# Score products of a chunked linear-attention head pair: five separate blocks on TensorE, or one of three and one of two

## The chip, the core and the metric

The kernel runs on one core of one Trainium2 chip. The metric is device time in microseconds (us). Engines are named as in the profile: PE is TensorE (matmuls), PEld its weight loads, DVE VectorE, ACT ScalarE, POOL GpSimd, SP SyncE (DMA queue). Each engine takes its instructions from a queue of its own, in order, and waits there for what an instruction needs.

## The reference

One layer of a decoder trunk on 1024 tokens of width 1024, in float32. RMS norm, then `proj = h @ w_in` into eight groups of 1024 columns (xa, ga, q, f, v, g, m_a, m_b). Two token mixers run side by side: an RG-LRU on xa, and an HGRN2 (gated linear attention, 8 heads of 128 channels) on q, f, v. They are gated, summed, multiplied by `w_out` and added to x; then a squared-ReLU MLP of width 4096, a residual and a last norm. The part in question is HGRN2, which the reference writes over chunks of 32 tokens:

```
rel    = cum[:, :, :, None, :] - cum[:, :, None, :, :]          # cum: running sum of log f
decay  = where(causal, exp(minimum(rel, 0.0)), 0.0)
scores = einsum('bhtsk,bhsk->bhts', qc[:, :, :, None, :] * decay, kc)
o      = einsum('bhtk,bhkv->bhtv', qc * exp(cum), state) + einsum('bhts,bhsv->bhtv', scores, vc)
state  = exp(last)[..., None] * state + einsum('bhsk,bhsv->bhkv', k_to_end, vc)
```

So the score of tokens t >= s is a sum over 128 channels of q(t), k(s) and the product of the gates f between s and t.

## The kernel before, in words

Tokens go in two chunks c of 512; heads go in four pairs p. For every (c, p) the kernel projects v, xa, q and f, runs the RG-LRU, then `hgrn` (L381 to L559), then `gates` (L561), which projects g, m_b, ga and m_a and joins the branches. There are eight such rounds, about 107 us each; then come the output projection and the MLP, which the change does not touch. A projection is 48 matmuls of 128x512, three for every float32 product split in two (`mm3`, L113 to L117, so L115, L116 and L117 in the profile); their PSUM tiles are `pj_f`, `pj_g`, `pj_mb`, `pj_ga`, `pj_ma`. The weights are split by ACT (L76, high part `wH`) and DVE (L77, low part `wL`).

`hgrn` has no exponentials: it multiplies gates into q and k, and gets the scores level by level:
- own level (L385 to L404): tokens in twos. `q1` holds three versions of q. 32 small matmuls (32 stationary columns, 48 moving columns, L394) give the block `sc1`; a product with mask `mf` (tile `dd`) and a predicated copy take it up.
- `LEVELS = (2, 8)` (L425 to L462): `qa` and `qb` hold seven versions of q for groups of four cells of 2 and of 8 tokens; 32 small matmuls each (`sc2`, `sc8`), and three predicated copies each into `dd` (L438). After each level k is multiplied in place by the gates behind it (`kk`, L448) and q by those ahead.
- 32 (L475 to L487, 16 matmuls at L479, `sc32`) and 64 (L488 to L500, 8 matmuls at L497, `sc64`); ACT copies these blocks into `scT`, and POOL copies `dd` into `scT` with four instructions (L466).

So the block of one level reads `kk` and q as that level left them, and the next level's products overwrite `kk`. After that come transposes of `kk` (L525, `pk`), `pkv` (L531), the outputs `po` (L538, L541), the states `sn` on DVE (L547), and squares on ACT (L551).

What sets the order: a scheduler places every instruction on its engine's queue when the program is built, from the order in which the source makes them, priorities (the RG-LRU has 300, weight splits 400) and its own estimate of when inputs are ready; only the instructions under `keep` (norms and splits in the first round and in `first_norm`) are held in source order. So projection matmuls of `gates` stand on PE between the five score blocks. `bank("sc")` and `bank("hg")` are two PSUM banks each, and `pj` four; `mt(tag, ...)` gives one SBUF buffer for each tag, so a tile waits for the last reader of the tile that had its tag before. The second chunk's norm (`first_norm(1)`: L136 on ACT, L137 on DVE, L138 on POOL, L139 on DVE) begins in the last round of the first chunk.

Of the kernel before, what the change touches and what calls it, by code (L numbers as in the profile page):

```python
# [18 lines left out]
P = 128  # L19
D = 1024  # L20
S = 1024
T = 512
# [11 lines left out]
LEVELS = (2, 8)  # L34
# [7 lines left out]
def trunk(ctx: ExitStack, tc: tile.TileContext, x, wts, mlp, pv, gains, mask_f, mask_u, out):  # L42
    nc = tc.nc
    V, A, G, PE = nc.vector, nc.scalar, nc.gpsimd, nc.tensor
# [13 lines left out]
    def bank(tag, name):  # L58
        return ps.tile([P, 512], F32, tag=tag, name=name, bufs={"pj": 4, "sc": 2, "hg": 2}[tag])
# [129 lines left out]
    t3, t4, t5, t6 = (par[:, i, :] for i in range(3, 7))  # L189
# [37 lines left out]
    scT = mt("scT", "scT", (P, 8, P))  # L227
# [128 lines left out]

    def q_of(c, p, pp):

        q1 = mt("q1", f"q1{c}{p}", (P, 1792))[:, 0:1536].rearrange("p (a b) -> p a b", b=3)
        sg = mt("tmp", f"sq{c}{p}", (P, 2, T))  # L360
        r2 = lambda a: a.rearrange("p (a b) -> p a b", b=2)
        for s in range(2):
            b = slice(256 * s, 256 * s + 256)
            A.activation(sg[:, s, :], pp[s], AF.Sigmoid)
            V.tensor_tensor(out=q1[:, b, 0:2], in0=r2(sg[:, s, :]), in1=r2(pp[s]), op=ALU.mult)
        return q1

    def f_of(c, p, pp):
# [9 lines left out]
        V.tensor_scalar(ff, ff, F_MIN, 1.0, op0=ALU.max, op1=ALU.min)  # L378
        return ff, kk

    def hgrn(c, p, q1, f, kk, v):  # L381

        nm = f"{c}{p}"
        mul = lambda o, a, b: V.tensor_tensor(out=o, in0=a, in1=b, op=ALU.mult)  # L384
        mul(q1[:, :, 2], q1[:, :, 1], f[:, 1::2])  # L385
        dd = mt("dd", f"dd{nm}", (P, 8, 32))

        def blocks(rhs, name):

            pt = bank("sc", f"sc{name}_{nm}")[:, : 8 * 48].rearrange("p (n t) -> p n t", n=8)  # L390
            for n in range(8):
                for b in range(4):
                    k = 4 * n + b
                    PE.matmul(  # L394
                        pt[32 * b : 32 * b + 32, n, :], kk[:, 32 * k : 32 * k + 32], rhs(k), start=True, stop=True
                    )
# [7 lines left out]
        V.copy_predicated(dd[:, :, 1::2], mu[:, 0, :, 1::2], pt[:, :, :, 2])  # L404

        seg = mt("seg", f"seg{nm}", (P, 1536))
        f4 = f.rearrange("p (a b c) -> p a b c", b=4, c=2)
        qa = mt("qa", f"qa{nm}", (P, 1792)).rearrange("p (a b c) -> p a b c", b=7, c=2)
# [2 lines left out]
            q1.rearrange("p (a b) c -> p a b c", b=4)[:, :, :, 0:3:2],  # L411
            f4[:, :, :, 0:1].to_broadcast([P, 128, 4, 2]),
        )
        mul(kk[:, 0::2], kk[:, 0::2], f[:, 1::2])
        t4 = seg[:, 0:512]
        mul(t4, f[:, 0::2], f[:, 1::2])
        qb = mt("q1", f"qb{nm}", (P, 1792)).rearrange("p (a b) -> p a b", b=56)
        off = 512

        def take(n):  # L420
            nonlocal off
            off += n
            return seg[:, off - n : off]

        for li, cw in enumerate(LEVELS):  # L425
            g = 256 // cw
            t4 = t4.rearrange("p (a b) -> p a b", b=4)
            q4 = qa if li == 0 else qb.rearrange("p a (b c) -> p a b c", c=cw)

            mul(q4[:, :, 5, :], q4[:, :, 3, :], t4[:, :, 2:3].to_broadcast([P, g, cw]))  # L430
            mul(q4[:, :, 4:7:2, :], q4[:, :, 2:6:3, :], t4[:, :, 1:2].unsqueeze(3).to_broadcast([P, g, 2, cw]))
            pt = blocks(lambda k: q4[:, k * g // 32 : (k + 1) * g // 32, 1:7, :], str(cw))
            pt = pt.rearrange("p n (a x) -> p (n a) x", x=6 * cw)
            dg = dd.rearrange("p n (a x) -> p (n a) x", x=4 * cw)
            for d, a in ((1, 0), (2, 3), (3, 5)):
                w = (4 - d) * cw
                m_ = mu[:, 3 * li + d, :, :].rearrange("p n (a x) -> p (n a) x", x=4 * cw)
                V.copy_predicated(dg[:, :, d * cw :], m_[:, :, d * cw :], pt[:, :, a * cw : a * cw + w])  # L438
# [8 lines left out]
            k4 = kk.rearrange("p (a b c) -> p a b c", b=4, c=cw)  # L447
            mul(k4[:, :, 0:3, :], k4[:, :, 0:3, :], after.unsqueeze(3).to_broadcast([P, g, 3, cw]))  # L448
            if li == 0:
                o4 = qb[:, :, 0:32].rearrange("p a (b x) -> p a b x", b=4)  # L450
                i4 = lambda j: qa[:, :, j, :].rearrange("p (a b) c -> p a b c", b=4)
                A.copy(o4[:, :, :, 0:2], i4(0))
                for j in range(1, 4):
                    m_ = t4[:, :, 0] if j == 1 else before[:, :, j - 2]
                    m_ = m_.rearrange("p (a b) -> p a b", b=4).unsqueeze(3).to_broadcast([P, 32, 4, 2])
                    mul(o4[:, :, :, 2 * j : 2 * j + 2], i4(j), m_)
            else:
                mul(q4[:, :, 1, :], q4[:, :, 1, :], t4[:, :, 0:1].to_broadcast([P, g, cw]))
                mul(q4[:, :, 2:4, :], q4[:, :, 2:4, :], before.unsqueeze(3).to_broadcast([P, g, 2, cw]))
            nxt = take(g)  # L460
            mul(nxt, before[:, :, 0], after[:, :, 1])
            t4 = nxt  # L462
        tc_ = t4
        qv = qb[:, :, 0:32]
        for b in range(4):
            G.tensor_scalar(  # L466
# [5 lines left out]
                op1=ALU.add,  # L472
            )

        pt = bank("sc", f"sc32_{nm}")[:, :256].rearrange("p (n t) -> p n t", n=8)  # L475
        for n in range(8):
            for b in (0, 2):
                k = 4 * n + b
                PE.matmul(  # L479
                    pt[32 * b : 32 * b + 32, n, :],  # L480
                    kk[:, 32 * k : 32 * k + 32],
                    qb[:, k + 1, 0:32],
                    start=True,
                    stop=True,
                )
        for b in (0, 2):
            A.copy(scT[32 * b : 32 * b + 32, :, 32 * b + 32 : 32 * b + 64], pt[32 * b : 32 * b + 32, :, :])  # L487
        q8 = qv.rearrange("p (a e) c -> p a e c", e=2)  # L488
        k8 = kk.rearrange("p (a e c) -> p a e c", e=2, c=32)
        t8 = tc_.rearrange("p (a e) -> p a e", e=2)  # L490
        mul(q8[:, :, 1, :], q8[:, :, 1, :], t8[:, :, 0:1].to_broadcast([P, 16, 32]))
        mul(k8[:, :, 0, :], k8[:, :, 0, :], t8[:, :, 1:2].to_broadcast([P, 16, 32]))
        t64 = take(16)
        mul(t64, tc_[:, 0::2], tc_[:, 1::2])
        pt = bank("sc", f"sc64_{nm}").rearrange("p (n t) -> p n t", n=8)
        for n in range(8):
            PE.matmul(  # L497
                pt[0:64, n, :], kk[:, P * n : P * n + 64], qb[:, 4 * n + 2 : 4 * n + 4, 0:32], start=True, stop=True
            )
        A.copy(scT[0:64, :, 64:128], pt[0:64, :, :])  # L500
        q16 = qv.rearrange("p (a e d) c -> p a e d c", e=2, d=2)
        k16 = kk.rearrange("p (a e c) -> p a e c", e=2, c=64)
        t16 = t64.rearrange("p (a e) -> p a e", e=2)
        mul(k16[:, :, 0, :], k16[:, :, 0, :], t16[:, :, 1:2].to_broadcast([P, 8, 64]))
        qf = mt("qa", f"qf{nm}", (P, 1792))[:, 0:1024]
        qf5 = qf.rearrange("p (a b c d) -> p a b c d", b=2, c=2, d=32)
        A.copy(qf5[:, :, 0, :, :], q16[:, :, 0, :, :])
        mul(
            qf5[:, :, 1, :, :],
            q16[:, :, 1, :, :],  # L510
            t16[:, :, 0:1].unsqueeze(3).to_broadcast([P, 8, 2, 32]),
        )
        t128 = take(8)
        mul(t128, t64[:, 0::2], t64[:, 1::2])

# [110 lines left out]
    for c in range(NC):  # L626
# [6 lines left out]
        for p in range(NPAIR):  # L633
# [6 lines left out]
            q1 = q_of(c, p, project(c, f"q{c}{p}"))  # L640
            f, kk = f_of(c, p, project(c, f"f{c}{p}"))
# [407 lines left out]
```

## Time and profile before

| | |
|---|---|
| median of 3 runs | 1620.1 us (1618.43 to 1620.38) |
| the profiled execution | 1621.31 us, of which its span (first to last instruction) is 1619.5 us |
| PE busy | 1573.0 us, 9240 matmul records |
| DVE busy | 1211.3 us, 1751 instructions |
| ACT busy | 763.0 us, 1186 instructions |
| POOL busy | 66.8 us, 99 instructions |
| mean granted TensorE clock | 0.996 |

The page of the profile lists busy time by engine, the costliest groups of instructions, and the chain that ended last. The view of waits lists who waited for whom. The timeline lists instructions by start; a row has start, duration, engine, line, operation, out<-in, shapes, and in brackets the idle time before it and what ended that. Matmuls are pipelined, so a PE row overlaps the next: on PE the distance from start to start is what counts.

### The profile page before, as it was taken

Reading aid. Unit: us, or ns where it says so; the run is one execution under the profiler, and the core shown is the slowest. Engines: PE = TensorE matmul, PEld = TensorE weight load, DVE = VectorE, ACT = ScalarE, POOL = GpSimd, SP = SyncE. Lnnn points to the kernel's source line nnn. Section 1 sums busy time; section 2 is a strip of 40 time slices with the busy share of each in tenths; the row PEclk is TensorE's granted clock in tenths of the full one; section 3 lists DMA queues with packets and bytes.
Section 4 is the critical chain, followed back from the end, with each engine's and each line's share of the span. In section 5 each row is a group of like instructions: output and inputs, shape, how many; then the busy total and the mean of one; then the engine's idle time right before and its main releaser. Section 6 shows DMA issues by size and latency. Waiting matters only on the chain.

```text
span 1619.5 us, 23177 instructions
## 1 busy us (share of the span) xinstructions
PE 1573.0 (97%) x9240; PEld 1302.9 (80%) x9240; DVE 1211.3 (75%) x1751; ACT 763.0 (47%) x1186; POOL 66.8 (4%) x99
## 2 busy tenths in 40 slices
PE   7999999999999999999999997999999999999998
PEld 6788788788788788788787875888888878888886
DVE  5975956848763865947758688888878888888876
ACT  4643545436433544446335466677667732222113
POOL 0010100100100000000100010000000000000000
PEclk9999999999999999999999999999999999999999
DMA  6212213122243212222122362666666575666652
GB/s 238 92 66 91 92 66 104 67 92 91 79 168 132 92 68 90 92 77 93 66 92 91 111 228 78 252 244 244 243 248 249 221 286 206 257 258 250 257 213 104
DMA packets 57996, 246.51 MB, mean 152 GB/s; under 512 B 6688, under 2 KB 6816, under 8 KB 47136
## 3 DMA queue, kind: packets, MB, share of 16 engines
q1 hardware_dynamic: 56304, 239.27, 39.6%
q10 hardware_dynamic: 1584, 5.77, 1.0%
q8 instruction: 72, 1.18, 0.3%
q14 instruction: 36, 0.29, 0.1%
HBM read 185.24 MB, written 59.77 MB: 151 GB/s over the span
## 4 chain that ended last, share of the span: by engine, by line
PE 77%; DVE 17%; DMA 2%; ACT 2%; issue 2%; POOL 0%; DVEq 0%; POOLq 0%; SPq 0%; ACTq 0%
PE dX L115 3%; PE dX L116 3%; PE dX L117 3%; PE uX L115 3%; PE uX L117 3%; PE uX L116 3%; DVE wL L77 2%; PE pj_ga L117 2%; PE pj_ga L116 2%; PE pj_ga L115 2%; PE pv L115 2%; PE pv L117 2%; PE pv L116 2%; PE pj_f L117 2%; PE pj_ma L117 2%; PE pj_ma L116 2%
## 5 line engine op out<-in xcount | busy, mean ns | idle before, releaser
L77 DVE TENSOR_TENSOR wL<-raw,wH 128x1024 fp32r<-128x1024 f32 x160 | 194.3, 1215 | 150.2 <-ACT wH L76 146.1
L76 ACT CAST wH<-raw 128x1024 fp32r<-128x1024 f32 x160 | 167.8, 1049 | 166.6 <-issue 66.5
L963 DVE TENSOR_TENSOR acc<-acc,dX 128x512 f32<-128x512 f32 x128 | 85.1, 684 | 29.5 <-PE dX L117 28.6
L76 ACT CAST wA<-q 128x512 fp32r<-128x512 f32 x32 | 19.8, 622 | 134.1 <-PE dX L117 101.5
L963 DVE TENSOR_TENSOR acc<-acc,dY 128x512 f32<-128x512 f32 x64 | 43.4, 686 | 15.6 <-PE dY L117 14.5
L345 DVE RECIPROCAL rr<-rr 128x512 f32<-128x512 f32 x16 | 53.5, 3346 | 0.0
L823 ACT ACTIVATE b<-b 128x512 f32<-128x512 f32 x48 | 30.2, 630 | 37.4 <-DVE b L822 37.4
L115 PE MATMUL pv<-wH,hT0H 128*128 128x256 f32 x128 | 37.4, 292 | 0.0
L116 PE MATMUL pv<-wL,hT0H 128*128 128x256 f32 x128 | 37.0, 289 | 0.0
L117 PE MATMUL pv<-wH,hT0L 128*128 128x256 f32 x128 | 37.0, 289 | 0.0
L115 PE MATMUL pv<-wH,hT1H 128*128 128x256 f32 x128 | 36.5, 285 | 0.0
L117 PE MATMUL pv<-wH,hT1L 128*128 128x256 f32 x128 | 36.2, 283 | 0.0
L116 PE MATMUL pv<-wL,hT1H 128*128 128x256 f32 x128 | 36.2, 283 | 0.0
L311 DVE SCALAR_TENSOR_TENSOR xc<-xp,pvt,xc 128x512 f32<-128x512 f32 x48 | 33.1, 747 | 0.0
L551 ACT ACTIVATE on<-po 128x128 f32<-128x128 f32 x64 | 16.9, 277 | 33.5 <-PE po L541 33.2
L570 ACT ACTIVATE smb<-pj_mb 128x512 f32<-128x512 f32 x16 | 9.6, 597 | 45.3 <-PE pj_mb L117 45.1
L824 ACT ACTIVATE b<-b 128x512 f32<-128x512 f32 x48 | 30.0, 630 | 1.1
L77 DVE TENSOR_TENSOR wA<-q,wA 128x512 fp32r<-128x512 f32 x32 | 22.0, 688 | 10.1 <-ACT wA L76 9.7
L444 POOL TENSOR_SCALAR seg<-seg 128x128 f32<-128x128 f32 (+1 forms) x16 | 14.5, 906 | 360.6 <-DVE seg L384 360.6
L565 ACT ACTIVATE g<-pj_g 128x512 f32<-128x512 f32 x16 | 9.6, 598 | 37.4 <-PE pj_g L117 37.4
L384 DVE TENSOR_TENSOR seg<-seg 128x128 f32<-128x128 f32 (+2 forms) x96 | 27.0, 311 | 0.2
L117 PE MATMUL pj_ga<-hT1H,wL 128*128 128x512 f32 x64 | 26.6, 415 | 0.0
(1854 smaller groups left out, 5251.7 us busy)
## 6 DMA issues: line engine op xcount, KB each, us to landing
raw<-wts_in SPq DMA_DIRECT2D x160, 512.0 KB, 3.4
q<-mlp_in SPq DMA_DIRECT2D x64, 512.0 KB, 4.0
x<-x_in SPq DMA_DIRECT2D x8, 512.0 KB, 6.5
acc<-x ACTq DMA_DIRECT2D x8, 512.0 KB, 5.4
y_out<-acc SPq DMA_DIRECT2D x16, 256.0 KB, 2.0
xs<-x_in SPq DMA_DIRECT2D x8, 256.0 KB, 3.5
x<-xs SPq DMA_DIRECT2D x8, 256.0 KB, 2.2
x2s<-x_in SPq DMA_DIRECT2D x4, 512.0 KB, 4.4
```

Of the source, the lines that this page charges most:

```text
L76: keep(A.copy(h, src))
L77: keep(V.tensor_tensor(out=lo, in0=src, in1=h.bitcast(F32), op=ALU.subtract))
L115: PE.matmul(o, ah, bh, start=first, stop=False, **how)
L116: PE.matmul(o, ah, bl, start=False, stop=False, **how)
L117: PE.matmul(o, al, bh, start=False, stop=last, **how)
L311: V.scalar_tensor_tensor(xc[:, s, :], xp[:, j : j + T], pvt[:, PV_CW + 8 * j + u : PV_CW + 8 * j + u + 1], xc[:, s, :], op0=ALU.mult, op1= ...
L345: V.reciprocal(rec, rec)
L384: mul = lambda o, a, b: V.tensor_tensor(out=o, in0=a, in1=b, op=ALU.mult)
L551: A.activation(on[:, 4 * s + n, :], po[:, n * P : (n + 1) * P], AF.Square, accum_out=ssq[:, 4 * s + n : 4 * s + n + 1])
L823: A.activation(b[:, at, :], b[:, at, :], AF.Relu, scale=-1.0 if at == 2 else 1.0)
L824: A.activation(b[:, at, :], b[:, at, :], AF.Square)
L963: V.tensor_tensor(out=dst, in0=dst, in1=banks[bk, pr], op=op)
```

## The change

The five blocks become two groups. Levels 1, 2 and 8 (`sc1`, `sc2`, `sc8`) are issued one behind another, held (by a dependency for the scheduler alone, no wait on the chip) behind the last q product of level 8. Then all mask products and predicated copies follow. Levels 32 and 64 (`sc32`, `sc64`) are issued as a second group behind the last q product of level 64. For that, each level's keys are kept: `kk` stays as it was for level 1, `kb` is new for level 2, `kc` for level 8 and 32 (tag `tmp`), and `kk` is written again for 64. `qb` gets a tag of its own instead of `q1`'s; `qf` takes the products of level 64. ACT gets the copies of what is not multiplied (`kb`, `kc`, `kk`). `sc8` goes to a bank of tag `hg`. The sums, products, masks and matmuls are otherwise those of before. The products `level_q` and `sums` are the former loop's, taken out as functions. The core of the diff, where the last pairs of lines but one are operands of the matmuls of `sc32` and `sc64`, each under `together(..., behind)`:

```diff
+    def together(ins, behind):
+        no_sync = mybir.DependencyInfo(mybir.DependencyClass.NoSync, mybir.DependencyReason.DATA)
+        tc.add_manual_dep(ins.ins, behind.ins.name, no_sync, reason="together")
...
-        def blocks(rhs, name):
+        def blocks(k_, rhs, name, behind, tag="sc"):
...
-        pt = blocks(lambda k: q1[:, 16 * k : 16 * k + 16, :], "1").rearrange("p n (a b) -> p n a b", b=3)
-        d2 = dd.rearrange("p n (a b) -> p n a b", b=2)
-        mf2 = mf.rearrange("p (a b) -> p a b", b=2).unsqueeze(1)
-        mul(d2, pt[:, :, :, 0:2], mf2.to_broadcast([P, 8, 16, 2]))
-        V.copy_predicated(dd[:, :, 1::2], mu[:, 0, :, 1::2], pt[:, :, :, 2])
+        def own_block(pt):
+            pt = pt.rearrange("p n (a b) -> p n a b", b=3)
+            d2 = dd.rearrange("p n (a b) -> p n a b", b=2)
+            mf2 = mf.rearrange("p (a b) -> p a b", b=2).unsqueeze(1)
+            mul(d2, pt[:, :, :, 0:2], mf2.to_broadcast([P, 8, 16, 2]))
+            V.copy_predicated(dd[:, :, 1::2], mu[:, 0, :, 1::2], pt[:, :, :, 2])
+        def level_blocks(li, cw, pt):
+            pt = pt.rearrange("p n (a x) -> p (n a) x", x=6 * cw)
+            dg = dd.rearrange("p n (a x) -> p (n a) x", x=4 * cw)
+            for d, a in ((1, 0), (2, 3), (3, 5)):
+                w = (4 - d) * cw
+                m_ = mu[:, 3 * li + d, :, :].rearrange("p n (a x) -> p (n a) x", x=4 * cw)
+                V.copy_predicated(dg[:, :, d * cw :], m_[:, :, d * cw :], pt[:, :, a * cw : a * cw + w])
...
-        mul(kk[:, 0::2], kk[:, 0::2], f[:, 1::2])
+        kb = mt("kb", f"kb{nm}", (P, 2 * T))
+        A.copy(kb[:, 1::2], kk[:, 1::2])
+        mul(kb[:, 0::2], kk[:, 0::2], f[:, 1::2])
...
-        qb = mt("q1", f"qb{nm}", (P, 1792)).rearrange("p (a b) -> p a b", b=56)
+        qb = mt("qb", f"qb{nm}", (P, 1792)).rearrange("p (a b) -> p a b", b=56)
...
-        for li, cw in enumerate(LEVELS):
...
+        level_q(qa, t4, g0, c0)
+        before, after = sums(t4, g0)
+        kc = mt("tmp", f"kc{nm}", (P, 2 * T))
...
+        A.copy(k4(kc, c0)[:, :, 3, :], k4(kb, c0)[:, :, 3, :])
+        mul(k4(kc, c0)[:, :, 0:3, :], k4(kb, c0)[:, :, 0:3, :], after.unsqueeze(3).to_broadcast([P, g0, 3, c0]))
...
+        behind = level_q(q4, t4, g1, c1)
+        pt1 = blocks(kk, lambda k: q1[:, 16 * k : 16 * k + 16, :], "1", behind)
+        pt2 = blocks(kb, lambda k: qa[:, k * g0 // 32 : (k + 1) * g0 // 32, 1:7, :], str(c0), behind)
+        pt8 = blocks(kc, lambda k: q4[:, k * g1 // 32 : (k + 1) * g1 // 32, 1:7, :], str(c1), behind, "hg")
+        before, after = sums(t4, g1)
+        own_block(pt1)
+        level_blocks(0, c0, pt2)
+        level_blocks(1, c1, pt8)
+        mul(k4(kc, c1)[:, :, 0:3, :], k4(kc, c1)[:, :, 0:3, :], after.unsqueeze(3).to_broadcast([P, g1, 3, c1]))
...
+        A.copy(pairs(kk)[:, :, 1, :], pairs(kc)[:, :, 1, :])
+        A.copy(pairs(qf)[:, :, 0, :], q8[:, :, 0, :])
+        mul(pairs(kk)[:, :, 0, :], pairs(kc)[:, :, 0, :], t8[:, :, 1:2].to_broadcast([P, 16, 32]))
+        behind = mul(pairs(qf)[:, :, 1, :], q8[:, :, 1, :], t8[:, :, 0:1].to_broadcast([P, 16, 32]))
...
+                        kc[:, 32 * k : 32 * k + 32],
+                        qb[:, k + 1, 0:32],
...
+                    pt64[0:64, n, :], kk[:, P * n : P * n + 64], qf[:, P * n + 64 : P * n + P], start=True, stop=True
...
+        mul(halves(kk)[:, :, 0, :], halves(kk)[:, :, 0, :], t16[:, :, 1:2].to_broadcast([P, 8, 64]))
+        mul(halves(qf)[:, :, 1, :], halves(qf)[:, :, 1, :], t16[:, :, 0:1].to_broadcast([P, 8, 64]))
```

More of the change, by code (lines that the diff above doesn't have):

```diff
@@ L423, in take, with sums @@
             return seg[:, off - n : off]
-        for li, cw in enumerate(LEVELS):
[L426 to L438, printed above, removed]
+        def sums(t4, g):
             after = take(3 * g).rearrange("p (a b) -> p a b", b=3)
@@ L446, in hgrn @@
             mul(after[:, :, 0], t4[:, :, 1], after[:, :, 1])
[L447 to L459, printed above, removed]
@@ new lines, in hgrn @@
+        A.copy(o4[:, :, :, 0:2], i4(0))
+        for j in range(1, 4):
+            m_ = t4[:, :, 0] if j == 1 else before[:, :, j - 2]
+            m_ = m_.rearrange("p (a b) -> p a b", b=4).unsqueeze(3).to_broadcast([P, 32, 4, 2])
+            mul(o4[:, :, :, 2 * j : 2 * j + 2], i4(j), m_)
+        nxt = take(g0)
+        mul(nxt, before[:, :, 0], after[:, :, 1])
+        t4 = nxt.rearrange("p (a b) -> p a b", b=4)
+        q4 = qb.rearrange("p a (b c) -> p a b c", c=c1)
+        behind = level_q(q4, t4, g1, c1)
@@ L478, in hgrn @@
                 k = 4 * n + b
[L479 to L485, printed above, removed]
+                together(
+                    PE.matmul(
+                        pt[32 * b : 32 * b + 32, n, :],
+                        kc[:, 32 * k : 32 * k + 32],
+                        qb[:, k + 1, 0:32],
+                        start=True,
+                        stop=True,
+                    ),
+                    behind,
+                )
@@ L489, in hgrn @@
[L489 to L492, printed above, removed]
+        A.copy(scT[0:64, :, 64:128], pt64[0:64, :, :])
         t64 = take(16)
         mul(t64, tc_[:, 0::2], tc_[:, 1::2])
[L495 to L499, printed above, removed]
```

55 lines of the change are left out of this document (33 added, 22 removed).

## The prediction

> **What bounds the kernel now.** First the page, for the bound as a whole.
>
> ```profile
> span 1619.5 us, 23177 instructions
> ...
> PE 1573.0 (97%) x9240; PEld 1302.9 (80%) x9240; DVE 1211.3 (75%) x1751; ACT 763.0 (47%) x1186; POOL 66.8 (4%) x99
> ...
> PE 77%; DVE 17%; DMA 2%; ACT 2%; issue 2%; POOL 0%; DVEq 0%; POOLq 0%; SPq 0%; ACTq 0%
> ```
>
> PE is busy nearly all the time, so a gain must come from time in which PE stands or is badly filled, and the change touches only the score blocks. Hence the view of waits, cut to PE:
>
> ```profile
> PE sc L394 <- DVE qb L384: 5.0, 8, 0.6
> PE sc L394 <- DVE q L384: 4.1, 8, 0.5
> ...
> PE sc L479 <- DVE qb L384: 0.4, 1, 0.4
> ```
>
> Two of the five blocks wait visibly for DVE in each of the eight rounds, 9.5 us in all. The timeline of PE in one round (second chunk, second pair) says more; all rounds repeat it closely.
>
> ```profile
> 654.13 0.39 PE L115 MATMUL pj_g<-hT1H,wH 128*128 128x512 f32 x1
> ...
> 664.56 0.39 PE L116 MATMUL pj_g<-hT1L,wH 128*128 128x512 f32 x1
> 665.46 0.89 PE L394 MATMUL sc<-q,kk 128*32 128x48 f32 x64 [0.51 <-DVE q L384]
> ...
> 670.26 0.39 PE L116 MATMUL pj_mb<-hT1L,wH 128*128 128x512 f32 x1
> 670.74 0.89 PE L394 MATMUL sc<-qa,kk 128*32 128x48 f32 x64
> ...
> 675.44 0.89 PE L394 MATMUL sc<-qb,kk 128*32 128x48 f32 x64 [0.62 <-DVE qb L384]
> ...
> 680.26 0.70 PE L479 MATMUL sc<-qb,kk 128*32 128x32 f32 x32
> ...
> 682.88 1.12 PE L497 MATMUL sc<-qb,kk 128*64 128x64 f32 x16
> ...
> 685.66 0.49 PE L117 MATMUL pj_ga<-hT1H,wL 128*128 128x512 f32 x1
> 685.99 0.39 PE L115 MATMUL pj_ga<-hT1H,wH 128*128 128x512 f32 x1
> ```
>
> From the first row to the second are 46 steps of projection matmuls: 10.43 / 46 = 0.227 us each. And now DVE beside it:
>
> ```profile
> 664.53 0.88 DVE L384 TENSOR_TENSOR q<-q,f 128x512 f32<-128x512 f32 x1
> ...
> 667.02 0.43 DVE L384 TENSOR_TENSOR dd<-sc,mf 128x256 f32<-128x256 f32 x1
> 667.35 1.22 DVE L77 TENSOR_TENSOR wL<-raw,wH 128x1024 fp32r<-128x1024 f32 x1
> 668.48 0.45 DVE L404 COPY_PREDICATED dd<-mu,sc 128x128 f32<-128x128 uint8 x1
> 668.71 0.74 DVE L384 TENSOR_TENSOR kk<-kk,f 128x512 f32<-128x512 f32 x1
> ...
> 669.98 0.70 DVE L384 TENSOR_TENSOR qa<-qa,seg 128x512 f32<-128x512 f32 x1
> ...
> 672.76 0.47 DVE L438 COPY_PREDICATED dd<-mu,sc 128x192 f32<-128x192 uint8 x1
> 673.06 0.97 DVE L384 TENSOR_TENSOR kk<-kk,seg 128x768 f32<-128x768 f32 x1
> 673.93 0.30 DVE L438 COPY_PREDICATED dd<-mu,sc 128x128 f32<-128x128 uint8 x1
> 674.13 0.43 DVE L384 TENSOR_TENSOR qb<-qb,seg 128x256 f32<-128x256 f32 x1
> 674.47 0.29 DVE L438 COPY_PREDICATED dd<-mu,sc 128x64 f32<-128x64 uint8 x1
> 674.60 0.69 DVE L384 TENSOR_TENSOR qb<-qb,seg 128x512 f32<-128x512 f32 x1
> ...
> 678.89 1.22 DVE L384 TENSOR_TENSOR qb<-qb,seg 128x256 f32<-128x256 f32 x2
> ...
> 682.65 0.68 DVE L384 TENSOR_TENSOR qf<-qb,seg 128x512 f32<-128x512 f32 x1
> 683.25 1.22 DVE L77 TENSOR_TENSOR wL<-raw,wH 128x1024 fp32r<-128x1024 f32 x1
> 684.39 0.69 DVE L384 TENSOR_TENSOR kk<-kk,seg 128x512 f32<-128x512 f32 x1
> ...
> 687.45 0.35 DVE L547 SCALAR_TENSOR_TENSOR sn<-scar,seg,pkv 128x128 f32<-128x128 f32 x1 [1.25 <-PE pkv L531]
> 687.84 0.73 DVE L547 SCALAR_TENSOR_TENSOR sn<-sn,seg,pkv 128x128 f32<-128x128 f32 x2
> ```
>
> Set the ends of DVE's products against the starts of the blocks: 665.41 and 665.46; 670.68 and 670.74; 675.29 and 675.44; 680.11 and 680.26. Blocks start 0.05 to 0.15 us behind the product that they read, also where the profile names no wait. **So the score blocks go at DVE's pace**, and DVE has no idle time from the first of these rows to the last but two. What the change does to PE's order matters less than when DVE ends the last product of each group.
>
> **Part by part.** The order of the built programs gives the counts. From the start of `pj_f` the old blocks stand behind 119, 137, 150, 166 and 173 projection matmuls; the new group of three behind 163, the group of two behind 183 (the same in seven rounds; 184 in the last of the first chunk). The number of matmuls and their shapes stay.
>
> *PE.* Three of five entries and exits go. An entry costs 0.48 us from start to start where no wait is named (670.26 to 670.74), 0.25 over a step; the first step behind a small run is 0.33 (685.66 to 685.99), 0.10 over. But an entry is a gain only if DVE is ready.
>
> *When DVE has the input of group two.* From 664.53 to 684.39 the old order spends 19.86 us, with no gap. It holds every instruction that the new order puts ahead of group two, the split of the weight at 683.25 too, which now stands ahead of the last products; and one more, the product `qf` for the halves, which takes 683.25 - 682.65 = 0.60 and now comes later. That leaves 19.26.
>
> *What is added on DVE: chains.* The mask product and the predicated copies all write `dd`, so each waits for the one before. Before, other products stood between them and the next instruction started early: 0.33 behind the mask product of 0.43, 0.23 behind the copy of 0.45, then 0.30, 0.20 and 0.13 behind copies of 0.47, 0.30 and 0.29. Now the five and a sixth stand in a row. What a chained pair costs is seen at 687.45: 0.35, and 0.04 later the next. So 0.10 + 0.22 + 0.17 + 0.10 + 0.16 + 5 x 0.04 = 0.95 us. The bounds are 0 and about 1.2 (a chained product of small sums too); I take 0.95, as the `sn` row shows just this case.
>
> [...]
>
> *The sum for group two.* 664.53 + 19.26 + 0.95 + 0.08 (the last product's own end: 0.68 against its step of 0.60) + 0.15 to PE = **684.97**. The old program reaches the 64-block at 682.88 behind 173 matmuls; ten more make 682.88 + 2.27 = **685.15**. Gain 0.18 us a round, in seven rounds 1.3.
>
> *Does PE get there first?* The last product of group one moves: ahead of it come a weight split (1.13, from 667.35 to 668.48), two gate products with g (some 0.6 each, as 682.65 to 683.25 for the same size) and two small sums (at most 0.3 together); five mask operations go behind it (0.33 + 0.23 + 0.30 + 0.20 + 0.13 = 1.19). So 674.60 + 1.4 + 0.69 + 0.15 = 676.9 for `sc8`; PE is there by 664.56 + 44 x 0.227 + 0.48 + two blocks of at most 0.89 = 676.8. With 0.89 for the block and twenty steps, PE stands before group two at about 682.5, DVE serves it at 685.0. The 2.5 us of stall take what the three entries and the two old waits gave, so no price of an entry or of a switch inside a group changes the result as long as it is below that.
>
> *Last round of the first chunk.* There the next norm falls into the chain:
>
> ```profile
> 418.36 0.14 DVE L137 TENSOR_SCALAR rstd_x<-rstd_x 128x1 f32<-128x1 f32 x1
> ...
> 423.23 1.28 DVE L139 SCALAR_TENSOR_TENSOR xn<-x,rstd_x,gain 128x1024 f32<-128x1024 f32 x1
> ```
> ```profile
> 418.64 1.01 POOL L138 TENSOR_TENSOR rstd_x<-rstd_x,mhalf 128x1 f32<-128x1 f32 x1 [0.23 <-DVE seg L384]
> ```
>
> Both DVE instructions now stand ahead of the mask product, with one small one between. DVE waits out POOL, 418.36 to 419.65 plus 0.15, less some 0.3 done meanwhile, 1.1; the norm product 1.2. In this round products stand between the copies again (some 0.6 of the chain back), and POOL's copies fall behind group two (up to 0.6 back). Net +1.1 to +1.7, against a gain of 0.18 and 0.36 of visible wait that this round had: about **0.8 us lost**.
>
> *Hidden work.* ACT gets three copies more a round:
>
> ```profile
> 673.29 1.05 ACT L76 CAST wH<-raw 128x1024 fp32r<-128x1024 f32 x1 [5.55 <-issue]
> ...
> 682.94 0.62 ACT L507 COPY qf<-qb 128x512 f32<-128x512 f32 x1
> ```
>
> Each is at most 0.62, and ACT idles 5.55 us there; the last that group two needs (`qf`) can start when `qb` is done, about 1.2 us before DVE's last product ends, so it is covered; without cover it would cost 0.62. Behind group two PE has four projections before `pk` instead of six, ACT makes the second `kT` behind one weight cast (1.05) that came later, while PE has ten matmuls for it instead of six (0.91 more): 0.1 us lost in each second-chunk round. In the first chunk PE's small runs split once or twice more, 0.10 each. Together about 0.8. SP's loads keep their order but for a few neighbours; weights are split before they are needed by more than 5 us.
>
> Total: -1.3 + 0.8 + 0.8 = **+0.3 us**. On the profiled span that is 1619.5 + 0.3 = 1619.8, its time 1621.6; the median shown is 1.2 us below that execution, so **1620.4 us**.
>
> **The rivals.** No change means within 0.2% (3.2 us), about what a measurement of this kernel can tell.
>
> *Chains cost nothing* (faster). Without the 0.95 the eight rounds gain 7.6 more: 1620.4 - 7.6 = 1612.8. It decides from 0.45 us a round. For it: a copy's duration in the row may hold time behind the instruction before it. Against: the `sn` rows. 0.17.
>
> *PE's switches are the limit, not DVE* (faster). [...] By rows: three entries of 0.25 and three exits of 0.10 and the two named waits (9.1 / 8 = 1.14) would go, 2.2 us a round, 17.5 in all: 1602.6. The 0.05 to 0.15 us between product and block, the same in all rounds, speak against it. 0.03.
>
> *POOL locks DVE out* (slower). POOL's four copies of `dd` now fall beside the split, and the last three products of group two:
>
> ```profile
> 679.14 2.16 POOL L466 TENSOR_SCALAR scT<-dd 32x256 f32<-32x256 f32 x4 [5.93 <-DVE dd L438]
> ```
>
> Beside them two products took 1.22 at 678.89; at 674.13 and 674.60 the same sizes made 0.34 + 0.69 = 1.03. So one of four copies cost 0.2, and the 19.86 holds that. [...] If DVE stood for all of the 2.16, less 0.2 to 0.8 held in the sum, a round would lose 1.4 to 2.0, all 11 to 16: 1631 to 1636; at half of it 1626. It decides from 0.4 us a round. 0.25 for at least that.
>
> *The change doesn't do what it says*: the built order on PE shows the blocks together, so nothing is given to it.
>
> **How the numbers follow.** Forecast 0.55, within 0.2%; faster 0.17 + 0.03 = 0.20; slower 0.25. Range: from the first rival to between the third's half and its full price, 1612.8 to 1628; own range of the forecast 1617.2 to 1623.6.
>
> **What would show it.** In the new profile: PE waiting at `sc8`, `sc32` or `sc64` for DVE, over 2 us a round; 0.15 us between DVE's last product and the 64-block; DVE with about 20.4 us from `q<-q,f` to that product's end, predicated copies 0.04 us behind each other; a longer wait in the last round of the first chunk. Wrong would be a second group that starts with no named wait (then entries count and it is faster), or copies of POOL over which `wL` and `kk` rows stretch (slower).

## The result, and the profile after

The changed kernel took 1627.5 us (median of 6 runs, 1624.7 to 1632.3) against 1618.5 us for the kernel before (6 runs, 1618.2 to 1620.4): a ratio of 1.005, 95% interval 1.004 to 1.0061. That lies inside the range, just below its upper end, and outside the forecast of no change. The profiled execution is the slowest of the six, 1632.3 us at a mean granted clock of 0.988; the other five had 0.991 to 0.993, so what follows is the dearest case.

From the page of the changed kernel (span; busy time by engine; the queue q8, which e2 and e8 tie to PE's instructions):

```profile
span 1630.5 us, 23238 instructions
...
PE 1577.3 (97%) x9240; PEld 1313.0 (81%) x9240; DVE 1216.0 (75%) x1751; ACT 775.5 (48%) x1210; POOL 63.7 (4%) x99
...
q8 instruction: 72, 1.18, 0.3%
```

The same 9240 matmul records take PE 4.3 us more, and the span grows by 11.0. So this is not only waiting: matmuls themselves got longer. (A small float32 matmul leaves two records, called passes here: the 32 matmuls of `sc8` are 64 passes.) The view of waits, PE of the changed kernel (engine, line, releaser: total us, times, longest):

```profile
PE sc L398 <- issue: 7.5, 4, 2.0
...
PE sc L525 <- DVE qf L388: 4.6, 5, 2.0
PE sc L513 <- DVE qb L388: 3.6, 4, 1.1
PE sc L398 <- DVE qb L388: 2.9, 8, 0.4
```

Before, the blocks waited 9.5 us for DVE. Now they wait 11.1 for DVE and 7.5 for "issue", that is, for nothing that the profile names. The two kinds stand in different places, as the timeline of PE shows. First chunk, first pair:

```profile
98.28 0.93 PE L513 MATMUL sc<-qb,kc 128*32 128x32 f32 x32 [1.04 <-DVE qb L388]
99.89 1.91 PE L525 MATMUL sc<-qf,kk 128*64 128x64 f32 x16 [0.67 <-DVE qf L388]
101.72 0.80 PE L115 MATMUL pj_ga<-hT0H,wH 128*128 128x512 f32 x1
102.32 0.63 PE L116 MATMUL pj_ga<-hT0L,wH 128*128 128x512 f32 x1
102.75 0.63 PE L117 MATMUL pj_ga<-hT0H,wL 128*128 128x512 f32 x1
...
684.63 0.63 PE L398 MATMUL sc<-qb,kc 128*32 128x48 f32 x40 [0.37 <-DVE qb L388]
687.23 0.71 PE L398 MATMUL sc<-qb,kc 128*32 128x48 f32 x24 [1.97 <-issue]
687.87 0.80 PE L116 MATMUL pj_mb<-hT1L,wH 128*128 128x512 f32 x1
```

Above the dots, PE stands before each half of group two and waits for DVE, as predicted. Behind it the projection steps are 0.43 us apart (102.32 to 102.75) instead of 0.227, and the 64-block takes 1.91 instead of 1.12. Below the dots is the second chunk, second pair (the round of the prediction): PE stops *inside* `sc8`, after 40 of its 64 passes, for 1.97 us, and the next projection is slow again, 0.80 instead of 0.39. The stretches of 3.41 us around both places, with busy time by engine and the granted clock in the last column but two:

```profile
96.51:99.92 3.41, 1.68 (x37) 1.06 (x36) 3.23 (x4) 1.22 (x3) 3.22 (x4) 1.00 0.43 143
99.92:103.33 3.41, 3.41 (x20) 3.00 (x21) 1.44 (x3) 1.79 (x4) 0.09 (x1) 0.50 0.04 16
683.60:687.01 3.41, 1.29 (x103) 1.05 (x90) 3.13 (x14) 0.00 (x0) 0.00 (x0) 1.00 0.27 106
687.01:690.43 3.42, 3.20 (x30) 2.60 (x31) 2.13 (x6) 0.45 (x1) 0.37 (x1) 0.50 0.02 5
```

PE is busy for 1.68 of 3.41 us, or 1.29, and in the 3.41 us that follow the clock is granted at 0.50. The changed kernel has such a stretch in each of the eight rounds; before, no round had one. At 0.50 a stretch of 3.41 us loses half of its work, some 1.7 us (an estimate). Over the whole of the prediction's round, `pj_f` to `poT`, the view of windows gives for before, then for changed:

```profile
637.56:710.76 73.20, 71.80 (x556) 58.31 (x555) 57.12 (x88) 36.47 (x64) 5.20 (x7) 1.00 0.22 76
645.39:720.27 74.88, 72.46 (x555) 59.62 (x554) 57.89 (x88) 37.97 (x67) 4.80 (x7) 0.98 0.23 73
```

Measured from the first matmul of `pj_f` to the first of `poT` (two rows of the timeline), a round takes:

| kernel | first chunk, us | second chunk, us |
|---|---|---|
| before | 74.0, 73.2, 73.2, 73.6 | 73.2, 73.2, 73.2, 73.3 |
| changed | 75.6\*, 74.8\*, 74.8\*, 75.2\* | 74.9\*, 74.9\*, 74.7\*, 74.9\* |
| e1, 80 passes between the chunks | 74.1, 74.8\*, 74.8\*, 75.2\* | 74.7\*, 74.6\*, 73.2, 73.2 |
| e2, 60 passes at the start | 75.6\*, 74.8\*, 75.0\*, 73.8 | 74.7\*, 74.8\*, 74.8\*, 73.2 |
| e3, group two later | 71.9, 71.1, 71.1, 71.1 | 75.1\*, 74.6\*, 74.8\*, 73.0 |
| e4, group one apart | 74.1, 73.3, 73.1, 73.2 | 73.0, 73.2, 73.2, 73.3 |
| e5, e3 and 80 passes | 71.9, 71.1, 71.1, 71.1 | 71.1, 71.1, 71.1, 71.1 |
| e6, e3 and group one split | 72.5, 71.6, 71.6, 71.6 | 71.5, 71.6, 71.6, 71.6 |
| e7, filled | 74.1, 73.3, 73.3, 73.7 | 73.1, 73.2, 74.1, 74.6\* |
| e8, a load held back | 74.0, 74.8\*, 73.2, 73.8 | 73.2, 73.2, 73.2, 73.8 |
| e9, five blocks held apart | 72.2, 71.4, 71.4, 71.9 | 71.4, 71.4, 71.5, 71.5 |

A star marks a round with half-clock time in it. The first round of all is some 0.8 longer in every kernel, and the last of the first chunk has the next norm in it. Of the others the table carries the case: 71.1 to 71.6 where the blocks wait for at most 0.6 in all, 73.2 with longer waits or a stall (before has its own), 74.8 with these and half clock behind them. (74.1 in e7 has a stall inside `sc8` and then waits of its own, without half clock.) The change's loss is the step from 73.2 to 74.8, eight times in this execution.

### The profile page after: what moved, and what is told of

It is laid out like the page before. It is cut to its first block, busy times and chain, and to the rows that moved or that the text cites. A ratio compares the mean times of both kernels' runs of the same rounds, so it can differ in the third digit from the quotient of the medians.

```text
span 1630.5 us, 23238 instructions
## 1 busy us (share of the span) xinstructions
PE 1577.3 (97%) x9240; PEld 1313.0 (81%) x9240; DVE 1216.0 (75%) x1751; ACT 775.5 (48%) x1210; POOL 63.7 (4%) x99
## 3 DMA queue, kind: packets, MB, share of 16 engines
q8 instruction: 72, 1.18, 0.3%
## 4 chain that ended last, share of the span: by engine, by line
PE 60%; DVE 10%; issue 1%; DMA 1%; ACT 1%; POOL 0%; DVEq 0%; POOLq 0%; SPq 0%; ACTq 0%
PE dX L115 3%; PE dX L116 3%; PE uX L115 3%; PE dX L117 3%; PE uX L117 3%; PE uX L116 3%; PE uY L117 2%; PE uY L116 2%; PE uY L115 2%; PE dY L116 2%; PE dY L115 2%; PE dY L117 1%; DVE wL L77 1%; PE po L116 1%; PE po L117 1%; PE po L115 1%
## 5 line engine op out<-in xcount | busy, mean ns | idle before, releaser
L77 DVE TENSOR_TENSOR wA<-q,wA 128x512 fp32r<-128x512 f32 x32 | 22.0, 687 | 11.3 <-ACT wA L76 11.1
L115 PE MATMUL pj_ga<-hT0H,wH 128*128 128x512 f32 x64 | 27.6, 431 | 0.0
L116 PE MATMUL pj_mb<-hT1L,wH 128*128 128x512 f32 x64 | 27.5, 429 | 0.0
L116 PE MATMUL pj_ga<-hT0L,wH 128*128 128x512 f32 x64 | 27.2, 425 | 0.0
L117 PE MATMUL pj_ga<-hT0H,wL 128*128 128x512 f32 x64 | 27.1, 423 | 0.0
L117 PE MATMUL pj_mb<-hT1H,wL 128*128 128x512 f32 x64 | 26.8, 418 | 0.0
```

Of the source, the lines that this page charges most:

```text
L77: keep(V.tensor_tensor(out=lo, in0=src, in1=h.bitcast(F32), op=ALU.subtract))
L115: PE.matmul(o, ah, bh, start=first, stop=False, **how)
L116: PE.matmul(o, ah, bl, start=False, stop=False, **how)
L117: PE.matmul(o, al, bh, start=False, stop=last, **how)
```

## The experiments

**Theory**: PE stands idle in one piece, in the first chunk for DVE, in the second because its instructions have not arrived, and the clock falls to half behind it. **Rivals**: the "issue" stall is a data wait that the profile misses; only the waits cost, not the clock; what stands behind group two is late.

**e1 and e2: move the instruction blocks.** The page's q8 row gives 1.18 MB / 72 = 16.4 KB a packet, and 9240 / 72 = 128 passes between two packets (with their weight loads, 18480 records of PE and PEld, 18480 / 72 = 257 instructions). In the four rounds of the second chunk the stall stands after 157, 168, 178 and 189 passes of group one, some 11 later each round, which no data explains, since each round has the same program. Small passes put in ahead should move it.

```
+    def small_passes(n):
+        pt = bank("hg", f"pad{n}")
+        for i in range(n // 2):
+            PE.matmul(pt[0:32, 0:48], ident[:, 0:32], ident[:, 0:48], start=True, stop=True)
...
+            small_passes(80)
```

In e1 the call stands ahead of the second chunk's rounds; in e2 it is `small_passes(60)` behind the first norm.

> The changed kernel with 40 tiny fp32 matmuls (80 passes of PE, 32x48, into a bank that nobody reads) between the two chunks. Theory 'instruction supply': PE's instructions come in blocks of 256, about 127 passes with their weight loads; in the second chunk a whole block lies inside group one (the stalls stand at passes 157, 168, 178 and 189 of its 192), and it runs out sooner than the next is there. 80 passes ahead move the boundaries to where the first chunk has them: no idle time put down to 'issue' inside sc8 in any round; PE then waits for DVE before group two in the second chunk as it does in the first (about 1.0 and 0.7 us). Time 1627 plus or minus 2 if half-clock windows follow these waits too, 1619 to 1621 if not. Rival 'hidden data wait' (kc or qb late, not recorded): the stalls stay at the same passes, 2.0 us each, in the same four rounds; 1628.

> The changed kernel with 30 tiny fp32 matmuls (60 passes) before the first round. Theory 'instruction supply': block boundaries of the first chunk (now about 92, 101, 111, 119 passes into group one) move to about 32, 41, 51, 59, so that a whole block lies inside the group: the first chunk gets stalls of about 2 us put down to 'issue', near passes 159, 168, 178 and 186; three of the four stalls of the second chunk go (its boundaries 30, 41, 51 become -30, -19, -9; the fourth comes to 2 and may stall again near pass 130). Rival 'hidden data wait': the first chunk has none, the second keeps its four at passes 157 to 189. Time about 1627 by both.

e1 took 1628.2 us (1.0058 of before, 1.0046 to 1.0071), e2 1632.2 (1.0074, 1.0061 to 1.0088). In e1 no "issue" is left, and PE waits for DVE in all eight rounds. In e2 the first chunk has the four stalls, after 158, 167, 176 and 185 passes, and the second chunk none. PE's timeline of e2, first round:

```profile
94.36 0.54 PE L398 MATMUL sc<-qb,kc 128*32 128x48 f32 x30 [0.37 <-DVE qb L388]
96.73 0.59 PE L398 MATMUL sc<-qb,kc 128*32 128x48 f32 x34 [1.83 <-issue]
```

In the changed kernel this round had no gap inside `sc8`; 60 tiny matmul passes that touch none of its data put one there, at the pass that the count gave. That PE runs out of instructions is thereby shown, and the hidden data wait has fallen. Neither run is faster, as expected: where the instructions come in time, PE waits for DVE instead. But e2 is 5 above the 1627 that was expected. Its profiled execution (1635.3) has two half-clock stretches behind the rounds that the changed kernel lacks, at 1022.5 and 1213.6 us, 3.4 us by the estimate above; whether they explain its median is not shown.

e1 shows one thing more. Its last two rounds have the same waits as the two before, but no half clock. PE's timeline of e1 in the third round of the second chunk, then stretches of 3.41 us, second and third round:

```profile
802.22 0.75 PE L513 MATMUL sc<-qb,kc 128*32 128x32 f32 x32 [1.03 <-DVE qb L388]
803.82 1.12 PE L525 MATMUL sc<-qf,kk 128*64 128x64 f32 x16 [0.85 <-DVE qf L388]
804.87 0.50 PE L115 MATMUL pj_ga<-hT1H,wH 128*128 128x512 f32 x1
805.20 0.40 PE L116 MATMUL pj_ga<-hT1L,wH 128*128 128x512 f32 x1
```
```profile
692.47:695.89 3.42, 1.70 (x47) 1.57 (x48) 2.43 (x4) 1.94 (x4) 2.51 (x4) 1.00 0.45 153
695.89:699.30 3.41, 3.41 (x14) 2.71 (x13) 2.43 (x3) 1.39 (x3) 0.00 (x0) 0.50 0.02 5
801.69:805.10 3.41, 2.03 (x49) 1.91 (x50) 2.05 (x4) 2.07 (x5) 2.13 (x3) 1.00 0.48 154
805.10:808.52 3.42, 3.42 (x23) 2.83 (x23) 2.91 (x5) 1.43 (x3) 0.00 (x0) 1.00 0.02 5
```

In the traces the clock changes only on a grid of 3.41 us, whatever the rounds do. In the changed kernel's, half clock lasts 3.413 us in each of the eight rounds and 6.827 us behind them, and its starts (from 99.92 to 994.21) lie 32, 32, 32, 44, 32, 32, 32 and 26 steps of 3.413 us apart; before's two starts (981.0 and 1011.8) lie 9 steps apart. The two places in e1 fit it: 805.10 - 695.89 = 109.21 us is 32.0 steps. In the second round the stall fell into one of its windows, PE was busy for 1.70 of 3.42, and the next window got half clock: 74.6 us. In the third round the grid cut the stall, the fuller window had 2.03, and the clock stayed: 73.2 us.

**e3: group two later.** `sc32` and `sc64` are held until 27 matmuls of `pj_ga` have been issued, so they stand behind 195 projection matmuls instead of 183 (184 in one round).

```
-        pa = project(c, f"ga{c}{p}")
+        pa = project(c, f"ga{c}{p}", group2, 27)
...
+                    at -= 3
+                    if at == 0:
+                        for ins in waiting:
+                            together(ins, last)
```

> The changed kernel with group two (sc32, sc64) held until 27 projection matmuls of pj_ga are issued: it stands behind 195 matmuls from pj_f instead of 183 in every round. Theory 'piled wait, then half clock': in the first chunk PE has projections to do until DVE is ready, so the waits of 1.0 and 0.7 us before sc32 and sc64 go and with them the half-clock windows that follow (1.7 us each): four rounds by 3.4 us, 13.6 less, 1614; the second chunk keeps its stall inside sc8 and its half-clock windows. Rival 'the waits alone cost': four rounds by 1.7, 6.8 less, 1621. Second rival 'what comes behind group two (scT, pk, kT, po) is then late': the gain is given back there, 1627 or more.

1615.3 us, 0.9973 (0.9964 to 0.9983): a miss by 1.3 for the theory, 5 to 6 for the rival, 12 for the second. PE's timeline, first round of e3:

```profile
99.50 0.39 PE L117 MATMUL pj_ga<-hT0H,wL 128*128 128x512 f32 x1
99.82 0.70 PE L517 MATMUL sc<-qb,kc 128*32 128x32 f32 x32
100.45 1.15 PE L529 MATMUL sc<-qf,kk 128*64 128x64 f32 x16
101.52 0.50 PE L115 MATMUL pj_ga<-hT0H,wH 128*128 128x512 f32 x1
```

No wait is named, the 64-block takes 1.15 again. The first chunk's rounds fall from 74.8 to 71.1; the second chunk's keep the stall inside `sc8`, the last of them without half clock. The rounds are measured to `poT`, so nothing behind group two was late.

**e4: group one apart.** The three blocks of group one run when they are ready (`together` is taken off them; behind 119, 134 and 147 matmuls); group two stays behind 183, the key copies stay.

```
-                    together(
                         PE.matmul(
                             pt[32 * b : 32 * b + 32, n, :], k_[:, 32 * k : 32 * k + 32], rhs(k), start=True, stop=True
-                        ),
-                        behind,
-                    )
+                    )
```

> The changed kernel with group one taken apart: sc1, sc2 and sc8 each run when their products are there (behind 119, 134 and 147 projection matmuls), the key copies stay, group two stays together behind 183. Theory 'instruction supply, then half clock': no run of 192 passes is left, so no idle time put down to 'issue', and no half-clock windows in the second chunk: 14 to 15 us less; two more entries a round give back 4; DVE's masks are not chained and it is ready for group two about 1 us sooner, which takes 2 to 9 from the first chunk. 1608 to 1615. Rival 'group two's waits or the key copies cost the time': within 3 us of the changed kernel, 1624 to 1631.

1618.5 us, 0.9995 (0.9986 to 1.0004). No issue stall and no half clock in any round, but 3.5 us or more above what was expected: its rounds take 73.2, as before. The waits tell why; PE of e4:

```profile
PE sc L401 <- DVE qb L392: 6.0, 8, 0.9
PE sc L401 <- DVE q L392: 4.1, 8, 0.5
PE sc L401 <- DVE qa L392: 2.8, 8, 0.5
```

Three blocks wait for DVE in each round, 12.9 us in all. Taken apart, but not held back, the blocks run into DVE's pace again. The rounds are as long as before although the key copies stay, so no price of these copies shows.

**e5 and e6: no long stall.** e5 is e3 with the 80 small passes of e1. e6 is e3 with `sc1` and `sc2` behind 139 matmuls and only `sc8` behind 162, so that group one is no longer one dense run.

```
-        level_q(qa, t4, g0, c0)
+        first = level_q(qa, t4, g0, c0)
...
-        pb = project(c, f"mb{c}{p}")
+        pb = project(c, f"mb{c}{p}", block8, 42)
```

> Group two held to 195 in every round, and the 80 small passes between the chunks. If the instruction supply, the piled wait and the clock behind both are all of the lost time: no 'issue' stall, no wait for DVE before group two and no half-clock window in any round; from pj_f to poT every round takes 71.1 (71.9 the first). Against the run with group two held alone, whose second-chunk rounds took 75.1, 74.6, 74.75 and 72.95: 4.0 + 3.5 + 3.65 + 1.85 = 13.0 less and 0.9 for the small passes: 1615.3 - 12.1 = 1603. Rival 'something else bounds the second chunk' (kT, pk, po, norm): rounds there stay above 73, 1609 or more.

> Group two held to 195, and group one taken in two: sc1 and sc2 behind 139 projection matmuls, sc8 behind 162. Theory 'instruction supply': with 23 projections (5.2 us) between them no block of 256 instructions is run through in less time than the next one takes to come, wherever its boundary lies: no 'issue' stall and no half-clock window without any shift; one more entry and exit a round, 0.35 each: 1615.3 - 13.0 + 2.8 = 1605. Rival 'the stall belongs to the data of sc8': it stays in the four rounds of the second chunk, 1617.

e5 took 1605.0 us, 0.991 (0.9897 to 0.9924); e6 1607.2, 0.9922 (0.9908 to 0.9935). Both within 2.2 us of what was expected, and both faster than either kernel. No half clock and no issue stall in any round, and e6 needs no small passes for it. One short wait is left in each round: 0.6 at `sc2` in e6, and in e5 at `sc8`, as its view of waits says:

```profile
PE sc L402 <- DVE qb L392: 3.0, 8, 0.4
```

**e7: useless work.** In the first chunk six full matmuls are put where PE stands idle; the true products overwrite them.

```
+        def fill(whole, count):
+            h = hT[c][0][0][:, 0, :]
+            for _ in range(count if c == 0 else 0):
+                together(PE.matmul(whole, h[:, 0:P], h, start=True, stop=True), behind)
+        whole = bank("sc", f"sc32_{nm}")
+        fill(whole, 4)
...
+        whole = bank("sc", f"sc64_{nm}")
+        fill(whole, 2)
```

> The changed kernel with useless work for PE: in the first chunk, four 128x512 fp32r matmuls ahead of sc32 into its bank and two ahead of sc64 into its bank, both overwritten afterwards; PE stands idle there now, waiting for DVE (1.0 and 0.7 us). Theory 'idle, then half clock': the window of 3.41 us no longer looks idle, and the half-clock window behind it goes: the four rounds fall from 74.8 (75.6 the first) to 73.2 (74.1): 6.3 less, 1621; the second chunk as in the changed kernel. Rival 'the clock costs nothing of its own, only the waits do': 1627 to 1629, the fill takes the place of idle time. If half-clock windows stay: about 1628.

1623.6 us (1.0025, 1.0015 to 1.0036). PE of e7, second round, then the window of its grid that holds most of it:

```profile
204.57 1.07 PE L511 MATMUL sc<-hT0H 128*128 128x512 f32 x4
205.71 0.70 PE L520 MATMUL sc<-qb,kc 128*32 128x32 f32 x32
206.33 0.73 PE L511 MATMUL sc<-hT0H 128*128 128x512 f32 x2
207.40 1.12 PE L534 MATMUL sc<-qf,kk 128*64 128x64 f32 x16 [0.33 <-DVE qf L388]
```
```profile
205.47:208.88 3.41, 3.01 (x53) 2.29 (x53) 2.05 (x4) 2.76 (x6) 1.93 (x3) 1.00 0.47 154
```

With work added, the first chunk's rounds go from 74.8 to 73.3 and none has half clock. In the second and third round the 64-block starts 47.6 us behind the start of `pj_f`, as in the changed kernel, so the fill took idle time alone: what the rounds gain behind it is the clock's, and the rival that the waits alone cost has fallen. The kernel is 3.9 us faster than the changed one by the medians, 2.6 above what was expected. In the second chunk the 24 added matmuls (six in four rounds) also moved the blocks, so the profile has fewer stalls there too; the first chunk's rounds are the clean part of this run, and not its whole time.

**e8: a load held back.** In the changed kernel 512 KB of weights land during group one. Here a one-element copy into the load's buffer, which reads `dd`, keeps them behind it:

```
+        if after is not None:
+            with tc.high_priority(400):
+                A.copy(raw[0:1, 0:1], after)
         nc.sync.dma_start(raw, wts[i])
...
+        held[used[0] + 9] = dd[0:1, 0, 0:1]
```

> The changed kernel with one weight load a round held back: in the changed kernel 512 KB for the next round land from 0.1 to 2.2 us after the start of group one, in all rounds, and the packet with the next instructions starts at 1.9 to 2.6 in the second chunk, when the load is through. Here a one-element copy on ACT into that load's buffer waits for the masks, and the load goes behind group one. Theory 'the instructions queue behind the load': their packet starts at 1.2 to 1.6, and the stall inside sc8 shrinks from 1.9 to 2.1 us to 0.9 to 1.3 in the second chunk; 3 less by that, 1624, and 6 less again if the half-clock windows there go, 1618. Rival 'a dense run is enough by itself': packet and stall as before, 1.9 to 2.1, 1627. Second rival 'the load is all of it': no stall at all.

1622.6 us (1.0023, 1.0013 to 1.0033), between the two numbers expected. DMA queues (packets, MB, share) of the changed kernel from 682.7 to 684.8, just behind the start of group one, then from 684.8 to 687.2; then of e8 from 1.1 to 2.2 us behind the start of its group one, in the same round:

```profile
q1 hardware_dynamic: 143, 0.52, 80.3%
```
```profile
q8 instruction: 1, 0.02, 2.4%
```
```profile
q8 instruction: 1, 0.02, 5.5%
```

And PE of e8 in that round:

```profile
678.34 0.63 PE L403 MATMUL sc<-qb,kc 128*32 128x48 f32 x40 [0.37 <-DVE qb L393]
679.86 0.46 PE L403 MATMUL sc<-qb,kc 128*32 128x48 f32 x24 [0.89 <-issue]
```

With the load in the way, no instruction packet moves before 684.8, 2.1 us behind the group's start. Without it the packet starts at 1.1, and the stall at the same pass is 0.89 instead of 1.97. The four together fall from 7.5 to 4.8 us; the fourth falls least, from 1.9 to 1.6, and its packet starts at 1.65 and takes 1.5. So the dense run and the load make the stall together, the load about half of it in this round. The second chunk has no half clock any more, and its rounds take 73.2 (73.8 the last) although they still stall: a stall under a DVE-paced round only replaces later waiting. In the first chunk three of four rounds lose their half clock as well, with waits like the changed kernel's (in the third round 1.02 and 0.90, against 1.08 and 0.90); there the grid cuts them, as in e1 (in the emptiest window of that round PE is busy for 1.90 of 3.41 us). So the time of e8 is not the load's alone; the stalls are what it shows.

**e9: what grouping is worth.** Three versions of the keys, all five blocks apart, each held until DVE is sure to be ready.

```
-        pb = project(c, f"mb{c}{p}")
+        pb = project(c, f"mb{c}{p}", ((6, held["1"]), (27, held["2"]), (42, held["8"])))
-        pa = project(c, f"ga{c}{p}")
+        pa = project(c, f"ga{c}{p}", ((21, group2[:16]), (27, group2[16:])))
```

> The three versions of the keys stay, but all five blocks stand apart, each held back until DVE is sure to be ready: behind 126, 147, 162, 189 and 195 projection matmuls. No wait for DVE, no dense run of 192. It tells what the entries are worth against the waits: with 0.35 us for an entry and exit (0.25 and 0.10 from the profile of before), a round takes 71.1 + 3 x 0.35 = 72.15 from pj_f to poT, and all 1605.0 - 0.9 + 8.4 = 1612.5. Rival 'only the waits for DVE cost, a switch is free': 71.1 a round, 1604. [...]

1605.5 us, 0.9912 (0.9899 to 0.9925), as fast as e5. PE of e9, second round, first block:

```profile
186.36 0.39 PE L117 MATMUL pj_mb<-hT0H,wL 128*128 128x512 f32 x1
186.68 0.89 PE L402 MATMUL sc<-q,kk 128*32 128x48 f32 x64
187.50 0.50 PE L115 MATMUL pj_mb<-hT0H,wH 128*128 128x512 f32 x1
187.83 0.40 PE L116 MATMUL pj_mb<-hT0L,wH 128*128 128x512 f32 x1
```

The entry is 0.32 from start to start, 0.09 above a step, and the first step behind the block is 0.33, 0.10 above. Rounds are 71.4 against e5's 71.1: three more entries and exits cost 0.3 net. But e5's rounds hold the wait of 0.37 at `sc8`, and e9's hold none (0.44 in one round alone). So an entry and exit cost some (0.3 + 0.37) / 3 = 0.2 (an estimate, and the rows agree), and a switch is not free: that rival came within 1.5 us because the wait that went paid for half of the switches. The expectation of 1612.5 fell, 7 too high: it took 0.35 a switch and built on e5's 71.1 without taking the wait out. Two groups instead of five blocks are worth some 2.7 us net in eight rounds; the rest of the 14 us between before and e5 comes from blocks that hardly wait.

## Why the prediction was right or wrong

*Score blocks go at DVE's pace*: right, and shown by e3, e4 and e9. With blocks that hardly outrun DVE (waits of at most 0.6 a round in all) a round takes 71.1 to 71.6; with blocks that do it takes 73.2, however they are grouped. The rival that PE's switches are the limit fell with e9, which has all five entries and is as fast as e5.

*The sum for group two*: right to 0.15. From the start of `pj_f` (637.56 in that round of before) the sum's 684.97 is 47.4; in the second and third round of the changed kernel, and in undisturbed rounds of e1, e7 and e8, the 64-block starts at 47.5 to 47.6. The old block's 45.3 and ten steps of 0.227 make 47.6. The forecast gain of 0.18 a round was nearly nothing, and nothing came: 73.2 and 73.2. The chain is in DVE's timeline, second pair of the second chunk, and the products ahead of group two in the first round are above it:

```profile
97.25 0.88 DVE L388 TENSOR_TENSOR qb<-qb,seg 128x512 f32<-128x512 f32 x1
98.06 0.88 DVE L388 TENSOR_TENSOR kk<-kc,seg 128x512 f32<-128x512 f32 x1
98.86 0.88 DVE L388 TENSOR_TENSOR qf<-qb,seg 128x512 f32<-128x512 f32 x1
...
685.17 0.42 DVE L388 TENSOR_TENSOR dd<-sc,mf 128x256 f32<-128x256 f32 x1
685.62 0.44 DVE L410 COPY_PREDICATED dd<-mu,sc 128x128 f32<-128x128 uint8 x1
686.16 1.09 DVE L418 COPY_PREDICATED dd<-mu,sc 128x192 f32<-128x192 uint8 x3
```

685.17 + 0.42 to 685.62 is 0.03, the pair behind it 0.10: chained operations follow behind the end, as assumed, and the first rival has fallen. In the first chunk three products beside POOL's copies take 0.88 instead of 0.69. The sum held 0.2 of these 0.6, so 0.4 a round were missed there, a fifth of the 2.16 that POOL takes before (its four copies stretch more, to 3.64 from 96.37 on); the start of the 64-block shows that other terms were a little too large. DVE is slowed beside POOL, but that it stands for all or half of the 2.16, as the third rival's prices have it, no run shows; the runs show these 0.6 us, and they do not make the loss: with them the rounds without half clock are as long as before.

*"The 2.5 us of stall take what the three entries and the two old waits gave, so no price of an entry or of a switch inside a group changes the result as long as it is below that"*: **here it failed.** The stall did take what was given, but it was counted as idle time only. In one piece it leaves a window of 3.41 us less than half full (PE busy for 1.05 to 1.68 us of it in the eight rounds), and the next window runs at half clock (0.50): 74.8 instead of 73.2. Eight times 1.6 is 12.8. The profiled executions differ by 1632.3 - 1621.3 = 11.0; the rest is that before has three half-clock windows behind its rounds (two from 981.0, one from 1011.8) and the changed kernel two (from 994.2), which gives back some 1.7. Before took its waits in pieces of at most 0.6, and no window of its rounds fell to half (the emptiest has PE busy for 2.65 of 3.41 us). The rows showed the total of the stall; the prediction did not ask in how many pieces it comes. No term and no rival of it held the clock, so that 1627.5 lies inside the range is luck: the upper end of 1628 was drawn for the third rival, which is not what made the loss.

*PE waits at group two in every round*: right in the first chunk, wrong in the second, where PE had to stop inside `sc8` for its instructions. "What would show it" gave over 2 us of wait a round at `sc8`, `sc32` or `sc64`; the total was right, the place and the cause were not.

*Last round of the first chunk*: 0.8 lost was too much. 73.7 to 73.8 in e7 and e8 against 73.6 before is 0.2. *Hidden work*, 0.8: not seen, rounds without half clock are as long as before. *Price of an entry*: 0.25 held DVE's delay in it; without it 0.09 (e9). The exit's 0.10 stands.

## What to carry to other kernels

When a change gathers small waits into one, ask what the engine's clock makes of the gap: worked out from these rows, a gap that left PE busy for 1.05 to 1.68 of 3.41 us cost about 1.6 us more a round (74.8 against 73.2). Blocks that outran their producer gained nothing from being grouped (73.2 us a round either way, without half clock); hold them behind work that is there anyway, which brought 0.8 to 0.9% here, in two groups, in three or as five blocks. A long run of tiny matmuls can use up instructions faster than they arrive, as 192 passes did here (stalls of 1.75 to 1.97 us), and more so beside a large load (1.97 against 0.89 with the load held back): put ordinary matmuls between them (with 23 between, in e6, no stall was left).

## What the runs showed of the hardware

- **Half clock followed windows that were at most half full.** Over the windows of the grid in the rounds of all eleven kernels, worked out from the rows of PE as busy time in each: of 25 windows with PE busy for at most 50.0%, 24 were followed by half clock; of all others none, though they begin at 50.3%. In the changed kernel eight windows of the rounds have 31 to 49%, all others 78% or more; in before none has less than 78%. This is a count over these runs; no experiment tried one filling after another.
- **The grid meets the round.** With half clock a round of the second chunk repeats after 109.06 us (first matmul of `pj_f` to the next round's), 31.95 windows of 3.413 (as measured above), so the window falls into nearly the same place each time; without, after 107.4 (before), 31.5 windows, and it jumps by half. That fits the wide spread of the changed kernel (1624.7 to 1632.3), but was not tried by itself.
- **PE ran out of instructions.** 192 passes at 11 ns (0.71 us for 64) take 2.1 us and need 192 / 128 = 1.5 packets of instructions, each of 16.4 KB. In the changed kernel's second chunk the packet that PE lacked started 1.9 to 2.6 us behind the start of group one and took 0.9 (DMA packets of the trace), and PE stood for 1.75 to 1.97 in this dense run beside a load; with the load held back (e8) the stall at the same pass of the prediction's round was 0.89.
